# Two forms of a small matrix-vector product at the head of a two-layer diffusion trunk

## The chip, the cores and the metric

The kernel runs on one core of a Trainium2 chip. The metric is the device time of one execution in microseconds (us). The core's engines work side by side, each through its own list of instructions: TensorE (PE, whose weight loads are shown apart as PEld), VectorE (DVE), ScalarE (ACT), GpSimd (POOL) and SyncE (SP), which issues the transfers from the chip's memory. An engine waits only where an instruction needs what another engine or a transfer has not finished.

## The reference

Two streams of 256 tokens with 1024 features, the latent one (L) and its context (C), pass through two layers of half-step SwiGLU, token mixer and half-step SwiGLU. Every sub-layer is preceded by an RMS norm, a scale and a shift, and followed by a gate; these come from one small product per layer, the modulation: two vectors (one per stream) times a 1024 x 9216 matrix, in fp32.

```python
    s_c = jax.nn.silu(c)
    s_cc = jax.nn.silu(c_ctx)[None]
    for i in range(DEPTH):
        ...
        ml = (s_c @ w_mod[i] + b_mod[i]).reshape(-1, 3, 3, D)
        h = gated_residual(h, ml, 0, swiglu(ada_in(h, norm_g[i, 0], ml, 0), ffn_w_in[i, 0], ffn_w_out[i, 0]), 0.5)
        ...
            mc = (s_cc @ w_mod[i] + b_mod[i]).reshape(-1, 3, 3, D)
            hc = gated_residual(hc, mc, 0, swiglu(ada_in(hc, norm_g[i, 0], mc, 0), ffn_w_in[i, 0], ffn_w_out[i, 0]), 0.5)

def ada_in(h, g, m, j):
    xn = rms_norm(h, g)
    return (xn * (1.0 + m[:, j, 1][:, None]) + m[:, j, 0][:, None]).astype(h.dtype)
```

## The kernel before, in words

All activations are held with features on the 128 partitions, as eight chunks of 128 features. The large products use a format in which a float32 is split into a high part and a low remainder (`whi`, `wlo` for weights, two `slot` tiles for activations); a product is three matmuls, high by high, high by low, low by high. Weights stream through two `raw` buffers; ACT rounds them to `whi` (a CAST) and DVE subtracts to get `wlo`. `mm` (L259 is its matmul) issues one matmul and then lets a planner, which keeps an estimate of each engine's time, slip background work between matmuls. In the first stage the planner is held off, and the instructions stand in the order in which the code names them.

The change is in that first stage, which ends when the first SwiGLU runs in its steady form. The modulation's columns come in blocks of 512 (`blk`). Shift and scale of the first sub-layer are the blocks 0 to 3: blocks 0 and 2 hold shift and scale of features 0 to 511, blocks 1 and 3 those of 512 to 1023. `start_loads` fetches a block as four quarters (`q`) of 512 KB. `mod` multiplies it, with 1024 inputs as eight chunks `kk`. Before, the vectors are the stationary side: four columns (two vectors and two columns of padding or of low parts) by 512 moving weight columns, which gives a 4 x 512 result.

- Block 0 and the first half of block 2 are plain fp32 (`sT`).
- The other half of block 2 and all of blocks 1 and 3 are first split (`high` on ACT, `low` on DVE), and `s_parts` holds the split vectors; each chunk is two matmuls.
- The result lies along one axis of four rows, so `mod_end` copies it out (ACT) and `turn` turns it with four matmuls against `C_PAIR`, after which two DVE additions write it to `modT`.

The transfers are issued by SP in the order of the calls from L1376: block 0, constants, stream L, block 2, first weight tile, stream C, second weight tile, blocks 1 and 3. Around the products stand the RMS norm of each stream (`first_squares` on ACT, `add_squares` on DVE, `first_rows` as two-column matmuls on TensorE, `rsqrt` as eight small DVE operations, `diagonal`, `columns`), and `norm_steps`, which makes the split activations of one chunk at a time: a DVE product `t`, an ACT step that gives the high part, a DVE step that gives the low part.

`between` then runs the first two weight tiles on features 0 to 511: `half(i, s)` is weight tile i on stream s, 24 matmuls of 256 columns. Its order is half(0, L), half(1, L), the norm of C, half(0, C), `mod(1)`, `mod(3)`, and half(1, C) around their two `turn` steps. The remaining chunks of features (`normed(..., range(4, KC))`) need blocks 1 and 3. All later work is the same code in both kernels.

Of the kernel before, what the change touches and what calls it, by code (L numbers as in the profile page):

```python
# [9 lines left out]
F32 = mybir.dt.float32  # L10
F32R = mybir.dt.float32r
I32 = mybir.dt.int32
AF = mybir.ActivationFunctionType
ALU = mybir.AluOpType
# [3 lines left out]
P = 128  # L18
D = 1024
KC = D // P  # L20
# [8 lines left out]
L, C = 0, 1  # L29
# [5 lines left out]
C_PAIR = 386  # L35
# [36 lines left out]
def trunk(ctx, tc, a):  # L72
    nc = tc.nc

    cpool = ctx.enter_context(tc.tile_pool(name="cpool", bufs=1))
# [13 lines left out]
    def slot(shape, dt=F32):  # L89
        t = slots.tile([P, 1024], dt, tag="slot", name=nm("slot"))  # L90
        dims = dict(zip("abc", shape[1:]))
        names = " ".join(dims)
        flat = t[:, :int(np.prod(shape[1:]))]
        return flat if len(dims) == 1 else flat.rearrange(f"p ({names}) -> p {names}", **dims)
# [9 lines left out]
    def t512(dt=F32):  # L104
        return tmp.tile([P, 512], dt, tag="t512", name=nm("t512"), bufs=5)
# [12 lines left out]
    def one():  # L118
        return ps_one.tile([P, 512], F32, tag="one", name=nm("one"))
# [11 lines left out]
    def account(e, reads, writes, us):  # L131
        start = now[e]
        for ap in reads:
            t, by = ready.get(key(ap), (0.0, e))
            start = max(start, t + (HOP if by != e else 0.0))
        now[e] = start + us
        for ap in writes:
            ready[key(ap)] = (now[e], e)
# [22 lines left out]
    V = Engine("dve", nc.vector, 0.06, 960.0)  # L161
    A_ = Engine("act", nc.scalar, 0.09, 1200.0)
# [9 lines left out]
    con = cpool.tile([P, C_W], F32, name="con")  # L172
    sT = cpool.tile([P, KC, 4], F32, name="sT")
    vec = cpool.tile([P, 48 + 8 + 16], F32, name="vec")
    bmod = cpool.tile([P, 2, 72], F32, name="bmod")
# [82 lines left out]
    def mm(out, lhsT, rhs, start, stop):  # L258
        nc.tensor.matmul(out, lhsT=lhsT, rhs=rhs, start=start, stop=stop)  # L259
        n = int(np.prod(rhs.shape[1:]))  # L260
        account("pe", [lhsT, rhs], [out], n / 2400.0 * (1 if rhs.dtype == F32R and n >= 256 else 4) + 0.0025)
        advance()
# [47 lines left out]
    def force(tile_no, part, half=1, earlier=True):  # L310


        while True:
            wanted = [x for x in soon if x[1] < tile_no and earlier or x[1] == tile_no and x[3] <= part and x[4] <= half]
            if not wanted:
                return
            soon.remove(wanted[0])
            wanted[0][2]()
# [72 lines left out]

    bg = bg_steps()

    s_parts = cpool.tile([P, KC, 4], F32R, name="s_parts")
    A_.copy(out=s_parts[:, :, 0:2], in_=sT[:, :, 0:2])
    V.tensor_tensor(out=s_parts[:, :, 2:4], in0=sT[:, :, 0:2], in1=s_parts[:, :, 0:2].bitcast(F32), op=ALU.subtract)

    blocks, highs, lows = {}, {}, {}  # L400

    def start_loads(blk):
        for q in range(4):
            blocks[blk, q] = slot([P, 2, 512])
            dma(out=blocks[blk, q], in_=a["wmod"][0, blk, q // 2][:, 2 * (q % 2):2 * (q % 2) + 2, :])

    def high(blk, q):
        highs[blk, q] = slot([P, 2, 512], F32R)
        A_.copy(out=highs[blk, q], in_=blocks[blk, q])

    def low(e, blk, q):
        lows[blk, q] = slot([P, 2, 512], F32R)
        e.tensor_tensor(out=lows[blk, q], in0=blocks[blk, q], in1=highs[blk, q].bitcast(F32), op=ALU.subtract)

    def mod(blk, midway={}):

        ps = one()[0:4, :]
        for q in range(4):
            if q in midway:
                midway[q]()  # L420
            for k in range(2):
                kk = 2 * q + k
                ends = dict(start=kk == 0, stop=False), dict(start=False, stop=kk == KC - 1)
                if (blk, q) in highs:
                    mm(ps, lhsT=s_parts[:, kk, :], rhs=highs[blk, q][:, k, :], **ends[0])
                    mm(ps, lhsT=s_parts[:, kk, :], rhs=lows[blk, q][:, k, :], **ends[1])
                else:
                    mm(ps, lhsT=sT[:, kk, :], rhs=blocks[blk, q][:, k, :], start=kk == 0, stop=kk == KC - 1)
        return lambda: mod_end(blk, ps)

    def mod_end(blk, ps):
        row = t512()
        A_.copy(out=row[0:4, :], in_=ps)

        def turn():
            pt = one()
            for c in range(4):
                mm(pt[:, 2 * c:2 * c + 2], lhsT=row[0:4, c * P:(c + 1) * P], rhs=con[0:4, C_PAIR:C_PAIR + 2], start=True, stop=True)
            for v in range(2):
                V.tensor_tensor(out=modT[:, 0, v, 4 * blk:4 * blk + 4], in0=pt[:, v:8:2], in1=bmod[:, 0, 4 * blk:4 * blk + 4], op=ALU.add)  # L440
                made.add((0, v, blk))

        return turn

    def mcol(l, v, j, w, kk=slice(0, KC)):
        c0 = (j * 3 + w) * KC
# [41 lines left out]
    def first_squares(s, k):  # L488

        sq = t512()  # L490
        A_.activation(out=sq, in_=h[s][:, k:k + 2, :].rearrange("p k t -> p (k t)"), func=AF.Square)
        return sq

    def add_squares(e, acc, sq, eps=0.0):
        e.scalar_tensor_tensor(out=acc, in0=sq, scalar=eps * D / P / 2, in1=acc, op0=ALU.add, op1=ALU.add)
        return acc

    def first_rows(acc):
        ps = one()
        for t in range(2):  # L500
            for i in range(2):
                mm(ps[:, 2 * t:2 * t + 2], lhsT=acc[:, i * S + t * P:i * S + t * P + P], rhs=con[:, C_MEAN:C_MEAN + 2], start=i == 0, stop=i == 1)
        return ps[:, 0:4:2], ps[:, 1:4:2]
# [41 lines left out]
    def norm_steps(l, j, s, xt, bc, ks, kk):  # L545
        aa = tiny.tile([P, KC], F32, tag="scl", name=nm("scl"), bufs=2)
        V.scalar_tensor_tensor(out=aa[:, kk], in0=mcol(l, s, j, 1, kk), scalar=1.0, in1=ng[:, l, j, kk], op0=ALU.add, op1=ALU.mult)
        low = []

        def step(k):  # L550
            if k is not None:
                hi, lo = xt[k // 2]
                o = (slice(None), k % 2, slice(s * S, s * S + S))
                t = t256()
                bb = mcol(l, s, j, 0, slice(k, k + 1))
                V.scalar_tensor_tensor(out=t, in0=h[s][:, k, :], scalar=aa[:, k:k + 1], in1=bc[:, :S], op0=ALU.mult, op1=ALU.mult)
                A_.activation(out=hi[o], in_=t, func=AF.Identity, bias=bb, scale=1.0)
            if low:
                low.pop()()
            if k is not None:  # L560
                low.append(lambda: V.scalar_tensor_tensor(out=lo[o], in0=t, scalar=bb, in1=hi[o].bitcast(F32), op0=ALU.add, op1=ALU.subtract))

        return [lambda k=k: step(k) for k in list(ks) + [None]]
# [827 lines left out]
    def diagonal(s):  # L1391
        diag[s] = rstd_diag(rsqrt(*rows[s]))
# [5 lines left out]
    sums_l = first_squares(L, 0)  # L1398
    for k in range(2, KC, 2):
        add_squares(V, sums_l, first_squares(L, k), EPS if k == 2 else 0.0)  # L1400

    def early():
        rows[L] = first_rows(sums_l)
        turn = end()
        for q in (2, 3):
            high(2, q)
            low(V, 2, q)
        diagonal(L)
        turn()

    end_2 = mod(2, {2: early})
    turn_2 = end_2()
    columns(L)
    turn_2()
    pump()
    xt = norm_tiles()
    force(0, 0, 0)
    sums_c = []
    for i, step in enumerate(norm_steps(0, 0, L, xt, scale[L], range(4), slice(0, 4))):
        step()  # L1420
        if i >= 2:
            sums_c.append(first_squares(C, 2 * len(sums_c)))
    sums_c.append(first_squares(C, 6))
    force(0, 1, 0)

    def between(banks, ws):

        half = lambda i, s, ks=range(4): abreast(xt, s, [(banks[i][s], ws[i])], ks, True)
        half(0, L)
        add_squares(V, sums_c[0], sums_c[1])  # L1430
        add_squares(V, sums_c[2], sums_c[3])
        add_squares(V, sums_c[0], sums_c[2], EPS)
        half(1, L)
        rows[C] = first_rows(sums_c[0])
        diagonal(C)
        for q in range(2):
            high(1, q)
        columns(C)
        for i, step in enumerate(norm_steps(0, 0, C, xt, scale[C], range(4), slice(0, 4))):
            step()  # L1440
            if i >= 2:
                low(V, 1, i - 2)
                if i < 4:
                    high(1, i)
        half(0, C)
        low(V, 1, 3)
        for q in range(4):
            high(3, q)
            low(V, 3, q)
        turn_1 = mod(1)()  # L1450
        force(1, 1)
        turn_3 = mod(3)()
        turn_1()
        half(1, C, range(1))
        turn_3()
        half(1, C, range(1, 4))
        for s in BOTH:
            normed(0, 0, s, xt, scale[s], range(4, KC))
        state["inside"] = False
# [112 lines left out]
```

## Time and profile before

| quantity | value |
|---|---|
| time, median of 3 runs | 1951.71 us (1951.39 to 1952.37) |
| time of the profiled execution | 1952.25 us |
| its span, first to last instruction | 1950.2 us |
| TensorE busy in the span | 1924.2 us (99%) |
| VectorE, ScalarE, GpSimd busy | 1352.0, 687.9, 73.0 us |
| read from memory | 276.11 MB, 142 GB/s over the span |
| mean granted TensorE clock | 0.994 of full speed |

The profiled execution lies 2.05 us outside its span, and 0.54 us above the median. Times in the rows are counted from the span's start. An fp32 matmul stands in the trace as two weight loads and two matmul records, a matmul in the split format as one of each. A busy TensorE is not one that does useful work all the time: the records of consecutive matmuls overlap, so what counts is the distance from start to start.

### The profile page before, as it was taken

The page shows a single profiled execution, that of the slowest core. Times are in us where ns is not written, and L with a number is a line of the kernel's source. Part 1 is how long each engine was busy: PE and PEld are TensorE (multiplying, and loading weights), DVE is VectorE, ACT ScalarE, POOL GpSimd, SP SyncE. Part 2 cuts the span into 40 slices and gives each one's busy share as a digit, 9 for nine tenths or more (in the row PEclk, how much of TensorE's full clock was granted, in tenths as well). Part 3 has the DMA queues.
Part 4 walks back from the last instruction along what each step waited for, and adds up shares of the span by engine and source line. Part 5 has one row for each costly group of instructions (what it writes and reads, how often), then busy time and mean ns, then how long its engine had stood idle before and what let it go on. Part 6 is the DMA issues. An engine that isn't in the chain of part 4 may idle for free.

```text
span 1950.2 us, 26148 instructions
## 1 busy us (share of the span) xinstructions
PE 1924.2 (99%) x10458; PEld 1661.8 (85%) x10458; DVE 1352.0 (69%) x2402; ACT 687.9 (35%) x1035; POOL 73.0 (4%) x108
## 2 busy tenths in 40 slices
PE   7999999999999999999999999999999999999998
PEld 4888888898888888888888889888888899989998
DVE  5576666678788888876666676767632588887665
ACT  5422232333323232342222223322222366665443
POOL 1000000010000000100000000000000101100000
PEclk8999999999999999999999999999999999999999
DMA  7334534434434434234353343555433345544553
GB/s 287 141 137 129 187 130 136 156 119 151 142 133 141 147 130 142 86 130 149 125 179 132 140 139 98 194 189 200 162 101 82 110 119 113 98 115 167 194 176 114
DMA packets 70090, 278.85 MB, mean 143 GB/s; under 512 B 23632, under 2 KB 23888, under 8 KB 52304
## 3 DMA queue, kind: packets, MB, share of 16 engines
q1 hardware_dynamic: 69968, 277.18, 43.5%
q8 instruction: 82, 1.34, 0.3%
q14 instruction: 40, 0.33, 0.0%
HBM read 276.11 MB, written 1.05 MB: 142 GB/s over the span
## 4 chain that ended last, share of the span: by engine, by line
PE 94%; DVE 3%; ACT 2%; DMA 1%; issue 0%; SPq 0%; DVEq 0%; ACTq 0%
PE pair L259 61%; PE one L259 32%; DVE slot L151 1%; PE one L265 1%; DMA slot<-in_wmod 1%; DVE t L151 1%; ACT slot L151 1%; DVE wlo L151 1%; ACT whi L151 1%; DVE few L151 0%; DMA raw<-in_nv 0%; ACT t L151 0%; DVE h L151 0%; PE pair L265 0%; SPq L166 0%
## 5 line engine op out<-in xcount | busy, mean ns | idle before, releaser
L259 PE MATMUL pair<-slot,whi 128*128 128x512 f32 (+2 forms) x4000 | 1039.1, 351 | 6.8 <-ACT slot L151 4.7
L259 PEld LDWEIGHTS pair<-slot,whi 128*128 128x128 f32 x4000 | 696.4, 190 | 104.3 <-ACT slot L151 5.4
L259 PE MATMUL pair<-slot,wlo 128*128 128x512 f32 (+2 forms) x2000 | 682.5, 350 | 0.1
L259 PE MATMUL one<-slot,whi 128*128 128x512 f32 (+1 forms) x1860 | 481.4, 347 | 0.0
L151 DVE TENSOR_TENSOR wlo<-raw,whi 128x1024 fp32r<-128x1024 f32 (+1 forms) x400 | 436.4, 1122 | 38.5 <-ACT whi L151 37.7
L151 ACT CAST whi<-raw 128x1024 fp32r<-128x1024 f32 (+1 forms) x400 | 365.0, 959 | 225.3 <-PE one L259 138.6
L259 PEld LDWEIGHTS pair<-slot,wlo 128*128 128x128 f32 x2000 | 372.9, 190 | 48.8 <-DVE wlo L151 0.4
L259 PEld LDWEIGHTS one<-slot,whi 128*128 128x128 f32 x1860 | 325.9, 189 | 43.4
L259 PE MATMUL one<-slot,wlo 128*128 128x512 f32 (+1 forms) x930 | 323.1, 347 | 0.0
L151 DVE SCALAR_TENSOR_TENSOR acc<-mraw,sT,acc 128x512 f32<-128x512 f32 x392 | 279.2, 750 | 17.1 <-DMA mraw<-in_wmod 15.9
L151 ACT ACTIVATE t<-pair 128x512 f32<-128x512 f32 x66 | 39.4, 597 | 442.9 <-PE pair L259 442.9
L259 PEld LDWEIGHTS one<-slot,wlo 128*128 128x128 f32 x930 | 176.1, 189 | 21.8
L151 DVE TENSOR_TENSOR t<-pair,t 128x512 f32<-128x512 f32 x66 | 45.6, 692 | 204.2 <-ACT t L151 204.2
L151 DVE TENSOR_TENSOR slot<-t,slot 128x512 fp32r<-128x512 f32 (+2 forms) x144 | 88.1, 612 | 64.8 <-ACT slot L151 63.4
L151 ACT CAST slot<-t 128x512 fp32r<-128x512 f32 (+2 forms) x144 | 79.4, 552 | 122.1 <-DVE t L151 121.7
L151 DVE SCALAR_TENSOR_TENSOR h<-one,gate,h 128x256 f32<-128x256 f32 x112 | 49.6, 479 | 103.6 <-PE one L259 103.4
L151 POOL TENSOR_TENSOR t<-t,t 128x256 f32<-128x256 f32 x47 | 39.4, 850 | 1708.4 <-ACT t L151 1286.9
L259 PE MATMUL pair<-whi,slot 128*128 128x512 f32 (+1 forms) x384 | 98.5, 339 | 0.0
L259 PE MATMUL one<-slot,slot 128*128 128x512 f32 (+1 forms) x432 | 89.8, 348 | 1.3 <-DVE slot L151 1.0
L151 ACT ACTIVATE t<-h 128x256 f32<-128x256 f32 (+1 forms) x88 | 36.9, 434 | 142.8 <-DVE h L151 129.3
L259 PEld LDWEIGHTS one<-slot,slot 128*128 128x128 f32 x432 | 69.9, 189 | 10.8 <-DVE slot L151 1.4
L259 PEld LDWEIGHTS pair<-whi,slot 128*128 128x128 f32 x384 | 67.2, 189 | 7.5
(100 smaller groups left out, 1077.8 us busy)
## 6 DMA issues: line engine op xcount, KB each, us to landing
raw<-in_win SPq DMA_DIRECT2D x88, 1024.0 KB, 4.9
mraw<-in_wmod SPq DMA_DIRECT2D x128, 512.0 KB, 4.7
raw<-in_wout SPq DMA_DIRECT2D x64, 704.0 KB, 4.2
slot<-in_wmod SPq DMA_DIRECT2D x16, 512.0 KB, 10.3
raw<-in_rv SPq DMA_DIRECT2D x8, 1024.0 KB, 4.8
raw<-in_rg SPq DMA_DIRECT2D x8, 1024.0 KB, 4.9
raw<-in_ro SPq DMA_DIRECT2D x8, 1024.0 KB, 4.9
slot<-in_ex SPq DMA_DIRECT2D x8, 512.0 KB, 6.0
```

Of the source, the lines that this page charges most:

```text
L151: getattr(self.real, op)(*args, **kw)
L259: nc.tensor.matmul(out, lhsT=lhsT, rhs=rhs, start=start, stop=stop)
L265: nc.tensor.transpose(out=out, in_=in_, identity=ident)
```

## The change

`mod` now makes the weights the stationary side: for each chunk and each 128 of the block's 512 columns, the 128 x 128 piece of weights is loaded, and the two vectors move past it, in plain fp32. That is 32 matmuls of two columns per block, and the result stands on the partitions as `modT` wants it. `s_parts`, `high`, `low`, `mod_end` with its copy, and the turning matmuls are gone. The order is written anew: `early` (the row sums of stream L) comes before the second quarter of block 2; the squares of C follow all norm steps of L; `first_rows` of C and the forced second half of weight tile 0 come before half(1, L); half(1, C) stands whole between `mod(1)` and `mod(3)`.

```diff
-    s_parts = cpool.tile([P, KC, 4], F32R, name="s_parts")
-    A_.copy(out=s_parts[:, :, 0:2], in_=sT[:, :, 0:2])
...
-        ps = one()[0:4, :]
+        ps = one()[:, 0:8]
         for q in range(4):
             if q in midway:
                 midway[q]()
             for k in range(2):
                 kk = 2 * q + k
-                ends = dict(start=kk == 0, stop=False), dict(start=False, stop=kk == KC - 1)
-                if (blk, q) in highs:
-                    mm(ps, lhsT=s_parts[:, kk, :], rhs=highs[blk, q][:, k, :], **ends[0])
-                    mm(ps, lhsT=s_parts[:, kk, :], rhs=lows[blk, q][:, k, :], **ends[1])
-                else:
-                    mm(ps, lhsT=sT[:, kk, :], rhs=blocks[blk, q][:, k, :], start=kk == 0, stop=kk == KC - 1)
-        return lambda: mod_end(blk, ps)
...
+                for c in range(4):
+                    mm(ps[:, 2 * c:2 * c + 2], lhsT=blocks[blk, q][:, k, c * P:c * P + P], rhs=sT[:, kk, 0:2],
+                       start=kk + c == 0, stop=kk == KC - 1 and c == 3)
+                    account("pe", [], [], 0.1)
+
+        def end():
             for v in range(2):
...
+    end()
 
     def early():
         rows[L] = first_rows(sums_l)
-        turn = end()
-        for q in (2, 3):
-            high(2, q)
-            low(V, 2, q)
         diagonal(L)
-        turn()
-
-    end_2 = mod(2, {2: early})
...
+    end = mod(2, {1: early})
     columns(L)
...
         add_squares(V, sums_c[0], sums_c[2], EPS)
+        rows[C] = first_rows(sums_c[0])
+        force(1, 1, 0)
+        diagonal(C)
         half(1, L)
...
         half(0, C)
...
-        turn_1 = mod(1)()
+        mod(1)()
         force(1, 1)
-        turn_3 = mod(3)()
-        turn_1()
-        half(1, C, range(1))
-        turn_3()
-        half(1, C, range(1, 4))
+        half(1, C)
+        mod(3)()
```

From the steady first SwiGLU on, every engine has the same instructions in the same order. The head of TensorE's list before, where `one_168` is the result of block 0, `one_188` that of block 2, `one_193` the row sums of L, and `one_221` the turned block 0:

```order
L259 MATMUL one_168<-slot_97,sT 4x512 x2
L259 MATMUL one_188<-slot_103,sT 4x512 x2
L259 MATMUL one_188<-slot_105,sT 4x512 x2
L259 MATMUL one_193<-con,t_27_177 128x2 x4
L259 MATMUL one_221<-con,t_33_198 128x2 x4
L259 MATMUL one_188<-slot_200,s_parts 4x512
L259 MATMUL one_188<-slot_202,s_parts 4x512
```

The same head in the changed kernel, with block 0 as `one_165`, block 2 as `one_211`, the row sums as `one_220`, and `one_262` the norm factors of L spread over the partitions:

```order
L259 MATMUL one_165<-sT,slot_94 128x2 x8
L259 MATMUL one_211<-sT,slot_100 128x2 x8
L259 MATMUL one_220<-con,t_27_198 128x2 x4
L259 MATMUL one_211<-sT,slot_102 128x2 x8
L259 MATMUL one_211<-sT,slot_104 128x2 x8
L259 MATMUL one_211<-sT,slot_106 128x2 x8
L259 MATMUL one_262<-t_35_235,con 128x128 x2
```

A quarter of a block was two fp32 matmuls of 512 columns, or four split ones; it is now eight of two columns, and the turn is gone. The row sums stand one quarter earlier.

The end of the stage on TensorE, changed kernel: `one_431` is block 1, `one_494` block 3, `pair_308` with `whi_269` and `wlo_270` is half(1, C), and `pair_307<-slot_275` the first matmul on features 512 to 1023.

```order
L259 MATMUL one_431<-sT,slot_120 128x2 x8
L259 MATMUL pair_308<-slot_271,whi_269 128x256
...
L259 MATMUL pair_308<-slot_273,wlo_270 128x256 x4
L259 MATMUL one_494<-sT,slot_122 128x2 x8
L259 MATMUL one_494<-sT,slot_124 128x2 x8
L259 MATMUL one_494<-sT,slot_126 128x2 x8
L259 MATMUL one_494<-sT,slot_128 128x2 x8
L259 MATMUL pair_307<-slot_275,whi_267 128x256
```

Before, half(1, C) stood behind both blocks and closed the stage; now block 3 stands directly ahead of the first matmul that needs it.

On DVE in the changed kernel, around the norm of C: `t_54_299` is the sum of its squares, `few_349` the start of `rsqrt`.

```order
L151 SCALAR_TENSOR_TENSOR t_54_299<-t_56_303,t_54_299 128x512
L151 TENSOR_TENSOR wlo_268<-raw_109,whi_267 128x1024
L151 TENSOR_TENSOR wlo_270<-raw_112,whi_269 128x1024
L151 TENSOR_SCALAR few_349<-one_336 128x2
```

Before, one such subtraction stood between the sums and `rsqrt`; now there are two, and the ten subtractions of `low` are gone.

## Rows read from the trace of the kernel before

**Rows 1.** Busy time by stretch (start:end, length, engines; last: clock, DMA, GB/s).

```profile
34.16:37.57 3.41, 1.47 (x11) 1.22 (x11) 1.83 (x11) 0.00 (x0) 0.00 (x0) 1.00 1.01 402
37.57:47.81 10.24, 8.18 (x30) 6.04 (x30) 9.99 (x14) 7.58 (x10) 0.00 (x0) 0.50 0.02 8
54.64:58.05 3.41, 3.41 (x28) 3.24 (x28) 0.95 (x7) 0.38 (x1) 0.00 (x0) 1.00 0.81 320
58.05:61.47 3.42, 3.42 (x19) 3.42 (x18) 3.00 (x9) 1.93 (x4) 0.00 (x0) 0.50 0.67 271
61.47:1940.00 1878.53, 1872.40 (x10231) 1630.63 (x10231) 1312.80 (x2313) 655.97 (x987) 64.40 (x79) 1.00 0.43 139
```

**Rows 2.** TensorE in order of time (start, length, operation, count, wait before it).

```profile
5.21 12.96 PE L259 MATMUL one<-slot,sT 128*4 128x512 f32 x24 [5.21 <-DMA slot<-in_wmod]
...
25.49 3.96 PE L259 MATMUL pair<-slot,whi 128*128 128x256 f32 x16 [1.51 <-ACT slot L151]
...
33.99 0.95 PE L259 MATMUL one<-con,t 128*128 128x2 f32 x8
...
44.28 1.91 PE L259 MATMUL pair<-slot,wlo 128*128 128x256 f32 x8
45.98 8.42 PE L259 MATMUL one<-slot,s_parts 128*4 128x512 f32 x32
...
56.22 1.05 PE L259 MATMUL one<-con,t 4*128 4x2 f32 x8
57.20 2.27 PE L259 MATMUL pair<-slot,whi 128*128 128x256 f32 x12
...
60.55 0.63 PE L259 MATMUL pair<-slot,whi 128*128 128x256 f32 x2
...
62.05 0.40 PE L259 MATMUL pair<-slot,whi 128*128 128x256 f32 x2
...
72.12 0.40 PE L259 MATMUL pair<-slot,whi 128*128 128x256 f32 x2
```

**Rows 3.** Groups of instructions up to 63 us (count, busy us, mean ns, idle).

```profile
L259 PE MATMUL one<-slot,s_parts 128*4 128x512 f32 x40 | 10.4, 419 | 0.0
L259 PE MATMUL one<-con,t 4*128 4x2 f32 x32 | 4.2, 249 | 0.0
```

**Rows 4.** Weight loads in order of time, single ones and one merged stream.

```profile
9.43 0.13 PEld L259 LDWEIGHTS one<-slot,sT 128*4 128x4 f32 x1 [0.72 <-issue]
10.28 0.09 PEld L259 LDWEIGHTS one<-slot,sT 128*4 128x4 f32 x1 [0.72 <-issue]
10.71 0.09 PEld L259 LDWEIGHTS one<-slot,sT 128*4 128x4 f32 x1 [0.34 <-issue]
...
14.32 0.08 PEld L259 LDWEIGHTS one<-slot,sT 128*4 128x4 f32 x1 [0.52 <-DMA slot<-in_wmod]
...
33.88 0.98 PEld L259 LDWEIGHTS one<-con,t 128*128 128x128 f32 x8
...
43.47 0.29 PEld L259 LDWEIGHTS pair<-slot,whi 128*128 128x128 f32 x1 [0.60 <-DVE slot L151]
43.64 0.33 PEld L259 LDWEIGHTS pair<-slot,whi 128*128 128x128 f32 x1
```

**Rows 5.** ACT and DVE in order of time, around the two norms.

```profile
18.18 1.04 ACT L151 CAST slot<-slot 128x1024 fp32r<-128x1024 f32 x1 [0.27 <-DMA slot<-in_wmod]
...
24.02 0.23 DVE L151 TENSOR_TENSOR modT<-one,bmod 128x4 f32<-128x4 f32 x2 [1.45 <-PE one L259]
...
24.41 0.87 DVE L151 SCALAR_TENSOR_TENSOR t<-h,scl,one 128x256 f32<-128x256 f32 x2
...
28.25 1.22 DVE L151 TENSOR_TENSOR wlo<-raw,whi 128x1024 fp32r<-128x1024 f32 x1
29.38 2.01 DVE L151 SCALAR_TENSOR_TENSOR t<-t,t 128x512 f32<-128x512 f32 x3
...
37.63 0.87 DVE L151 SCALAR_TENSOR_TENSOR t<-h,scl,one 128x256 f32<-128x256 f32 x2 [0.54 <-PE one L259]
```

More of the change, by code (lines that the diff above doesn't have):

```diff
@@ L392, in trunk @@
     bg = bg_steps()
-    s_parts = cpool.tile([P, KC, 4], F32R, name="s_parts")
-    A_.copy(out=s_parts[:, :, 0:2], in_=sT[:, :, 0:2])
-    V.tensor_tensor(out=s_parts[:, :, 2:4], in0=sT[:, :, 0:2], in1=s_parts[:, :, 0:2].bitcast(F32), op=ALU.subtract)
-    blocks, highs, lows = {}, {}, {}
+    blocks = {}
     def start_loads(blk):
@@ L405, in start_loads @@
             dma(out=blocks[blk, q], in_=a["wmod"][0, blk, q // 2][:, 2 * (q % 2):2 * (q % 2) + 2, :])
[L407 to L413, printed above, removed]
     def mod(blk, midway={}):
-        ps = one()[0:4, :]
+        ps = one()[:, 0:8]
         for q in range(4):
@@ L422, in mod @@
                 kk = 2 * q + k
-                ends = dict(start=kk == 0, stop=False), dict(start=False, stop=kk == KC - 1)
-                if (blk, q) in highs:
-                    mm(ps, lhsT=s_parts[:, kk, :], rhs=highs[blk, q][:, k, :], **ends[0])
-                    mm(ps, lhsT=s_parts[:, kk, :], rhs=lows[blk, q][:, k, :], **ends[1])
-                else:
-                    mm(ps, lhsT=sT[:, kk, :], rhs=blocks[blk, q][:, k, :], start=kk == 0, stop=kk == KC - 1)
-        return lambda: mod_end(blk, ps)
[L431 to L438, printed above, removed]
+                for c in range(4):
[3 more added lines that the diff above has]
+        def end():
             for v in range(2):
-                V.tensor_tensor(out=modT[:, 0, v, 4 * blk:4 * blk + 4], in0=pt[:, v:8:2], in1=bmod[:, 0, 4 * blk:4 * blk + 4], op=ALU.add)
+                V.tensor_tensor(out=modT[:, 0, v, 4 * blk:4 * blk + 4], in0=ps[:, v:8:2], in1=bmod[:, 0, 4 * blk:4 * blk + 4], op=ALU.add)
                 made.add((0, v, blk))
-        return turn
+        return end
     def mcol(l, v, j, w, kk=slice(0, KC)):
@@ L1400, in trunk @@
         add_squares(V, sums_l, first_squares(L, k), EPS if k == 2 else 0.0)
+    end()
     def early():
         rows[L] = first_rows(sums_l)
-        turn = end()
-        for q in (2, 3):
-            high(2, q)
-            low(V, 2, q)
         diagonal(L)
-        turn()
-    end_2 = mod(2, {2: early})
-    turn_2 = end_2()
+    end = mod(2, {1: early})
     columns(L)
-    turn_2()
+    end()
     pump()
@@ L1417, in trunk @@
     force(0, 0, 0)
-    sums_c = []
-    for i, step in enumerate(norm_steps(0, 0, L, xt, scale[L], range(4), slice(0, 4))):
+    for step in norm_steps(0, 0, L, xt, scale[L], range(4), slice(0, 4)):
         step()
-        if i >= 2:
-            sums_c.append(first_squares(C, 2 * len(sums_c)))
-    sums_c.append(first_squares(C, 6))
     force(0, 1, 0)
+    sums_c = [first_squares(C, k) for k in range(0, KC, 2)]
     def between(banks, ws):
@@ L1432, in between @@
         add_squares(V, sums_c[0], sums_c[2], EPS)
+        rows[C] = first_rows(sums_c[0])
+        force(1, 1, 0)
+        diagonal(C)
         half(1, L)
[L1434 to L1437, printed above, removed]
         columns(C)
-        for i, step in enumerate(norm_steps(0, 0, C, xt, scale[C], range(4), slice(0, 4))):
+        for step in norm_steps(0, 0, C, xt, scale[C], range(4), slice(0, 4)):
             step()
[L1441 to L1444, printed above, removed]
         half(0, C)
[L1446 to L1449, printed above, removed]
-        turn_1 = mod(1)()
-        force(1, 1)
-        turn_3 = mod(3)()
-        turn_1()
-        half(1, C, range(1))
-        turn_3()
-        half(1, C, range(1, 4))
+        mod(1)()
+        force(1, 1)
+        half(1, C)
+        mod(3)()
         for s in BOTH:
```

## The prediction

> **What bounds the kernel now.** I read the busy time by stretch first. From 61.47 us on TensorE is busy in 1872.4 of 1878.5 us [rows 1], and from there every engine has the same list in both kernels. So the change is worth the shift of the moment at which TensorE reaches the first matmul on features 512 to 1023, 60.55 us before [rows 2], and of what the clock does just behind it; nothing later has slack to absorb a delay. Second, TensorE in order of time, to see what that moment hangs on. Two chains lead there: block 0, block 2 and norm of L up to the first wide matmul at 25.49; then half(0, L), half(1, L), norm of C, half(0, C) up to the modulation at 45.98 [rows 2]. Third, the weight loads, since the added matmuls are little else.
>
> **What goes and what comes on TensorE.** Gone are 24 records of the plain four-column form (12.96 us) [rows 2], 40 of the split form (10.4) and 32 turning ones (4.2) [rows 3], together 27.6 us. Added are 4 x 32 fp32 matmuls, 256 records, each with a full weight load and two columns. The form stands in the trace as the row sums: eight loads 0.98 us long, one taking 0.19, so they start 0.113 apart [rows 4], in a stretch whose granted clock is 1.00 [rows 1]. At that pitch a block is 64 x 0.113 = 7.2 us.
>
> At the lower level (1.2 GHz) there is no such row. The nearest is a pair of loads of the same size at 43.47 and 43.64, 0.17 apart [rows 4], clock 0.50 [rows 1]. The bounds are 0.113 (the clock doesn't matter) and 0.226 (all of it doubles); I take 0.17, the measured pair, and a block is 10.9 us. A wide split matmul is 0.120 at the high level (84 records from 62.05 to 72.12 [rows 2]) and 0.213 at the low one (eight in 1.91, the last 0.415 long [rows 2]).
>
> In the Trainium skill, "TensorE: Matmul & The Clock Gate", section "LDWEIGHTS (loading the stationary operand)", a load takes its columns divided by 1.2 in ns, 107 ns for 128, with no word of the gate. The trace agrees at the high level (0.113) and not at the low one (0.17); by the rule the sum would be that of rival 2.
>
> **Which level.** The first records start at the low level: 9.43 to 10.28 is 0.85 us for a record that takes 0.43 from 10.28 on [rows 4], so 5.1 us of wide work from 5.21 on raised the clock. It then falls after narrow work even without a gap: from 54.64 to 58.05 TensorE was busy all 3.41 us, with eight two-column records from 56.22 to 57.20 in it [rows 2], and from 58.05 the clock is 0.50 [rows 1]; wide work alone (256 or 512 columns), from 57.20, brought it back at 61.47, 4.3 us. So I take it that two-column streams let the clock fall and don't raise it, and blocks 0 and 2, now all of that form, never leave the low level. After the last wide work at 33.99 [rows 2] the high level lasted to 37.57 [rows 1], 3.6 us.
>
> The Trainium skill, same page, section "Why this matters for your kernels", asks that TensorE be kept busy without gaps to reach and hold the high clock. By that the gapless two-column streams would hold it, which the stretch before 58.05 contradicts; the time it gives is rival 1.
>
> **Chain of L.** Block 0 from 5.2 (its first quarter lands then) to 16.1. Quarter 0 of block 2 has landed (14.32 [rows 4]): 16 x 0.17 = 2.7, to 18.8. Row sums, 8 x 0.17 = 1.4, to 20.2. Three quarters, 8.2, to 28.4; the last one was in by 18.18 [rows 5], so no transfer is waited for. DVE's `rsqrt` hides under them. `columns` about 0.75, DVE's `t` at 29.2. Before it was at 24.41 and the first wide matmul 1.08 later [rows 2, 5]: now 30.3, which is 4.8 late.
>
> **Chain of C.** Before, `wlo` ended 5.06 after `t` and the sums of C 6.98 after it (28.25 + 1.22, 29.38 + 2.01 [rows 5]). ACT's squares no longer stand between L's steps, which returns 0.3: 34.0 and 35.9. Row sums of C to 37.3, half(1, L) 24 records, 2.9 to 5.1, to 40.2 to 42.4. Moving the row sums ahead of half(1, L) costs TensorE a short wait and buys the chance to hide `rsqrt`; but two `wlo` subtractions stand ahead of it on DVE (35.8 + 1.13 + 1.22 = 38.2), and before it took 2.7 from the row sums' end (33.99 + 0.95) to `t` at 37.63 [rows 2, 5]: 40.9, just as late as TensorE allows (40.2 + 0.75). So `t` of C is at 41.0 to 43.2. half(0, C) took 8.35 from `t` (to 45.98), with two `low` subtractions between the norm steps on DVE and the casts on ACT. Without them it is 1.08 + DVE's pace + 8 low-part matmuls: 5.0 with the clock high, 1.08 + 24 x 0.213 = 6.2 low. That is where taking out `high` and `low` pays, 2.2 to 3.4 us; the rest of them lay beside other work. `mod(1)` starts at 46.0 to 49.3, middle 47.7, against 45.98: 1.7 late.
>
> **End of the stage.** Before, 45.98 to 60.55 = 14.57. Now `mod(1)`: if the clock is high, 3.6 us for 32 records, then 32 x 0.17 = 5.4, together 9.0; if low 10.9; half each, 10.0. half(1, C) at the low level, 24 x 0.213 = 5.1. That is about what raises the clock (4.3 to 5.1), so `mod(3)` begins high in four cases of five: 9.4. Then a new wait: block 3 now stands directly ahead of the matmuls that need it, and what half(1, C) hid lies bare, from `modT` at 24.02 to the first matmul at 25.49, 1.5 us [rows 2, 5]; queued behind that matmul is everything else of TensorE. Sum 26.0, so 11.4 more.
>
> **Behind it.** After `mod(3)` the clock is low, and 4.3 to 5.1 us of wide work raise it: some 22 records x (0.213 - 0.120) = 2.1, less the 0.9 us of that kind that before had too (0.4): 1.7.
>
> **Sum.** 1.7 + 11.4 + 1.7 = 14.8 us on the profiled execution's 1952.25, which is 1950.2 of span and 2.05 around it, and 0.5 above the median of 1951.7. Forecast 1966.5. Its own range, with the two clock states in the middle (3 us down, 4.6 up) and the low pitch 0.02 either way (4 us), is 1959 to 1974.
>
> **Rivals.** I call less than 0.2% either way (1947.8 to 1955.6) the same, since no more can be told.
> 1. *The narrow streams hold the clock.* Place: blocks 0 and 2; it decides if the granted clock is 1.00 from about 10.3. Then block 0 is 30 records at 0.17 and 34 at 0.113, to 14.1; block 2 waits for its load as before (14.32); `t` of L is near 23.7, `t` of C 35.1, half(0, C) ends at 40.1, and 7.2 + 2.9 + 7.2 + 1.5 follow: 58.9, and no slow stretch behind it: 2 us gained, 1949.6, not slower. Against it stands the fall at 58.05; for it, that those narrow matmuls used four rows of the array, and that 1 us of row sums at 33.99 alone shows nothing. 9%.
> 2. *The load doesn't follow the clock.* 0.113 throughout, wide work still slow: `t` of L 23.7, `t` of C near 36.2, half(0, C) to 41.8, then 7.2 + 5.1 + 7.2 + 1.5: 62.8, and 1.7: 3.9 more, 1955.6. Against it the pair at 43.47; for it, that a pair is not a stream. 8%.
> 3. *The narrow records double.* 0.226: 136 records of the L chain, 8 of C's row sums and some 75 of blocks 1 and 3 at 0.055 more, 12 us: 1978.5. For it, that wide records nearly double (0.120 to 0.213). 12%.
>
> **Chances.** Forecast 68%, the rivals 9, 8 and 12, the rest (a wait that I don't see) 3. Leaving out rival 1 and the upper half of rival 3, the range is 1955 to 1978. Faster: a small part of rival 1, 0.04. Same: the rest of it and half of rival 2, 0.10. Slower: 0.86.
>
> **What would show it.** Right: clock 0.50 from the first record up to about 30 us; 64 records of block 0 in about 10.9 us; first wide matmul near 30; `mod(1)` starting near 47.7; a gap of 1.5 us behind `mod(3)`; the first matmul on features 512 to 1023 near 73.7. Wrong: a block in 7.2 us with the clock at 1.00 (rival 1) or 0.50 (rival 2), in 14 us (rival 3), or a transfer that ends a wait in blocks 0 or 2.

## The result, and the profile after

The changed kernel takes 1974.56 us (median of 4 runs, 1973.96 to 1975.11), the one before 1951.9 (4 runs, 1951.39 to 1952.37): a ratio of 1.0117, 95% interval 1.0103 to 1.013. The profiled execution took 1974.81 us, its span 1972.4; against 1952.25 of before that is 22.6 more, where the forecast had 14.8 more and a range that ended at 1978. The direction and the fall of the clock are as forecast; the size, which hangs on what a load costs at the lower level of the clock, is not.

TensorE in order of time in the changed kernel (start, length, operation, count, wait before it):

```profile
5.26 17.20 PE L259 MATMUL one<-sT,slot 128*128 128x2 f32 x80 [5.26 <-DMA slot<-in_wmod]
22.32 1.85 PE L259 MATMUL one<-con,t 128*128 128x2 f32 x8
24.03 10.38 PE L259 MATMUL one<-sT,slot 128*128 128x2 f32 x48
34.27 1.20 PE L259 MATMUL one<-t,con 128*128 128x128 f32 x4
36.58 4.09 PE L259 MATMUL pair<-slot,whi 128*128 128x256 f32 x16 [1.11 <-ACT slot L151]
...
43.38 2.16 PE L259 MATMUL pair<-slot,whi 128*128 128x256 f32 x16
...
48.32 3.38 PE L259 MATMUL pair<-slot,whi 128*128 128x256 f32 x16 [1.11 <-ACT slot L151]
51.54 1.12 PE L259 MATMUL pair<-slot,wlo 128*128 128x256 f32 x8
52.49 10.68 PE L259 MATMUL one<-sT,slot 128*128 128x2 f32 x64
63.03 3.47 PE L259 MATMUL pair<-slot,whi 128*128 128x256 f32 x16
66.33 1.12 PE L259 MATMUL pair<-slot,wlo 128*128 128x256 f32 x8
67.29 11.72 PE L259 MATMUL one<-sT,slot 128*128 128x2 f32 x64
80.52 1.10 PE L259 MATMUL pair<-slot,whi 128*128 128x256 f32 x2 [1.51 <-ACT slot L151]
...
94.90 0.63 PE L259 MATMUL pair<-slot,whi 128*128 128x512 f32 x2
```

The reader is to compare three moments with [rows 2]. The first wide matmul is at 36.58, was at 25.49: 11.1 late. `mod(1)` starts at 52.49, was 45.98: 6.5 late, so 4.6 were given back between the two. The first matmul on features 512 to 1023 is at 80.52, was 60.55: 20.0 late. A further 2.4 comes behind it: from there to the next stage's first matmul (94.90) pass 14.38 us, before 11.93 (60.55 to 72.48). From that matmul to the end of the span both kernels take the same, 1877.5 and 1877.7 us. On TensorE no transfer ends a wait after the first record.

Busy time by stretch (start:end, length, PE, PEld, DVE, ACT, POOL; then clock, DMA share, GB/s), which answers to [rows 1]:

```profile
52.49:55.75 3.26, 3.26 (x32) 3.26 (x31) 0.00 (x0) 0.00 (x0) 0.00 (x0) 1.00 0.00 0
55.75:63.03 7.28, 7.28 (x37) 7.28 (x36) 0.00 (x0) 0.00 (x0) 0.00 (x0) 0.50 0.00 0
...
65.99:69.40 3.41, 3.41 (x32) 3.41 (x31) 0.00 (x0) 0.00 (x0) 0.00 (x0) 1.00 0.65 271
69.40:86.47 17.07, 15.56 (x72) 15.24 (x72) 6.78 (x19) 3.72 (x8) 0.00 (x0) 0.50 0.00 1
86.47:1960.00 1873.53, 1866.98 (x10191) 1625.66 (x10190) 1309.20 (x2304) 654.13 (x984) 63.48 (x79) 1.00 0.43 140
```

`mod(1)` begins with the granted clock at 1.00 and loses it after 3.26 us, with TensorE busy in all of them; from 69.40, 2.1 us into `mod(3)`, and over the wait behind it the clock is at 0.50. From 86.47 on the clock is back at 1.00, as from 61.47 before. The first change of the clock that this trace records is at 42.10, to 1.00; what stands ahead of it has to be read from the records themselves. The weight loads, the first two singly, the first 80 merged, and `mod(1)` on either side of the fall (start, length), which answers to [rows 4]:

```profile
5.23 0.29 PEld L259 LDWEIGHTS one<-sT,slot 128*128 128x128 f32 x1 [5.23 <-issue]
5.39 0.34 PEld L259 LDWEIGHTS one<-sT,slot 128*128 128x128 f32 x1
...
5.23 17.14 PEld L259 LDWEIGHTS one<-sT,slot 128*128 128x128 f32 x80 [5.23 <-issue]
...
52.49 3.33 PEld L259 LDWEIGHTS one<-sT,slot 128*128 128x128 f32 x29
55.62 7.46 PEld L259 LDWEIGHTS one<-sT,slot 128*128 128x128 f32 x35
```

Over the first 80 loads the distance is 0.213 (17.14 less one load of 0.29, over 79). In `mod(1)` it is 0.11 while the clock reads 1.00 (29 in 3.33) and 0.21 while it reads 0.50 (35 in 7.46). So the stream from 5.23 on ran at 1.2 GHz. The first two loads start 0.16 apart but end 0.21 apart (5.52 and 5.73): only the start of the second is early.

DVE around the norms, which answers to [rows 5]:

```profile
35.51 0.87 DVE L151 SCALAR_TENSOR_TENSOR t<-h,scl,one 128x256 f32<-128x256 f32 x2 [0.71 <-PE one L259]
...
42.27 2.35 DVE L151 TENSOR_TENSOR wlo<-raw,whi 128x1024 fp32r<-128x1024 f32 x2
44.54 0.15 DVE L151 TENSOR_SCALAR few<-one 128x2 int32<-128x2 int32 x1
...
47.24 0.87 DVE L151 SCALAR_TENSOR_TENSOR t<-h,scl,one 128x256 f32<-128x256 f32 x2 [0.60 <-PE one L259]
...
79.05 0.23 DVE L151 TENSOR_TENSOR modT<-one,bmod 128x4 f32<-128x4 f32 x2 [14.48 <-PE one L259]
```

`t` of L is at 35.51 (24.41 before), `t` of C 11.73 later (13.22 before). The step `rsqrt` of C begins at 44.54, behind the two `wlo`. And 14.48 us in which DVE waits for TensorE end with block 3's result at 79.05.

### The profile page after: what moved, and what is told of

Same layout as the page of the kernel before. It is cut to its first block, busy times and chain, and to the rows that moved or that the text cites. A ratio compares the mean times of both kernels' runs of the same rounds, so it can differ in the third digit from the quotient of the medians.

```text
span 1972.4 us, 26437 instructions
## 1 busy us (share of the span) xinstructions
PE 1947.9 (99%) x10618; PEld 1703.8 (86%) x10618; DVE 1339.8 (68%) x2391; ACT 676.0 (34%) x1020; POOL 70.7 (4%) x108
## 4 chain that ended last, share of the span: by engine, by line
PE 95%; DVE 2%; ACT 1%; DMA 1%; issue 0%; DVEq 0%; SPq 0%; ACTq 0%
PE pair L259 61%; PE one L259 34%; PE one L265 1%; DVE slot L151 1%; DVE t L151 1%; DVE wlo L151 1%; ACT whi L151 0%; ACT slot L151 0%; DMA raw<-in_wout 0%; DMA raw<-in_nv 0%; DVE h L151 0%; DMA slot<-in_wmod 0%; ACT t L151 0%; DVE few L151 0%; PE pair L265 0%
```

## The experiments

Theory A: the price is TensorE's clock; streams of two moving columns leave it at 1.2 GHz or let it fall there, and that doubles the distance of the loads. Theory B: the price is the 256 full weight loads as such. Theory C: the price is the new order, above all block 3 directly ahead of the matmuls that need it. All six kernels compute the whole of the reference. The first four were timed on one chip together (before: 1951.88, 15 runs), the last two on another (1951.63, 18 runs).

**The same loads with 128 moving columns.** The moving side is the two vectors repeated 64 times; order, loads and their number are those of the changed kernel.

```diff
+    MW = 128
...
-        ps = one()[:, 0:8]
+        ps = one()[:, 0:4 * MW]
...
-                    mm(ps[:, 2 * c:2 * c + 2], lhsT=blocks[blk, q][:, k, c * P:c * P + P], rhs=sT[:, kk, 0:2],
...
+                    nc.tensor.matmul(ps[:, MW * c:MW * c + MW], lhsT=blocks[blk, q][:, k, c * P:c * P + P], rhs=s_wide[:, kk, :],
...
+    s_wide = slot([P, KC, MW])
+    V.tensor_copy(out=s_wide.rearrange("p k (n v) -> p k n v", v=2), in_=sT[:, :, 0:2].unsqueeze(2).broadcast_to([P, KC, MW // 2, 2]))
```

> The changed kernel with one size altered: the moving side of the 128 modulation matmuls is 128 columns wide (the two vectors, repeated 64 times by one DVE copy ahead of the stage) in place of 2; the same 256 weight loads, the same order. Theory A (the two-column stream lets the granted clock fall, and the load's pitch is 0.213 us at the low level and 0.112 at the high one): the clock reads 1.00 from about 10 us on, block 0 takes 24 records at 0.213 and 40 at 0.115, 9.7 us, the later blocks about 7.4 each, first wide matmul near 25, time 1948 to 1954 us. Theory B (256 full weight loads are the price, and the clock is a bystander): the records stay 0.21 apart or get slower, time 1974 us or more.

Measured: 1952.95 (1950.67 to 1956.63, 11 runs), ratio to before 1.001 [1.0001, 1.0019]. Of the 22.7 us, 21.6 are gone. TensorE in order of time, and the stretches:

```profile
4.96 11.56 PE L412 MATMUL one<-slot,slot 128*128 128x128 f32 x80 [4.96 <-DMA slot<-in_wmod]
...
24.79 3.96 PE L259 MATMUL pair<-slot,whi 128*128 128x256 f32 x16 [1.13 <-ACT slot L151]
...
40.70 7.31 PE L412 MATMUL one<-slot,slot 128*128 128x128 f32 x64
...
59.53 0.91 PE L259 MATMUL pair<-slot,whi 128*128 128x256 f32 x2 [1.51 <-ACT slot L151]
```

```profile
5.00:9.57 4.57, 4.57 (x21) 4.57 (x22) 0.00 (x0) 0.00 (x0) 0.00 (x0) 1.00 0.95 306
9.57:26.64 17.07, 15.59 (x129) 14.67 (x128) 7.28 (x26) 6.52 (x12) 6.55 (x25) 1.00 1.02 415
...
40.70:47.76 7.06, 7.06 (x66) 7.06 (x65) 0.00 (x0) 0.00 (x0) 0.00 (x0) 1.00 0.02 8
```

Up to 9.57, ahead of the first recorded change, 21 records take 4.57 us, 0.218 each, against 0.213 in the changed kernel (the stretch holds 22 loads, so a record more or less is the whole difference); then the clock goes up and a block takes 7.31, 0.11 a record. 64 times the columns cost nothing at either level, so it is not the moving columns that set the distance; the loads are what the two forms share. With the wide form the clock came up after 9.57 and stayed over `mod(1)`, where the two-column form lost it. It was not at 1.00 throughout, as the expectation had it: two stretches of 3.4 us, from 26.64 and from 60.77, read 0.50. B falls: the loads are all there, and the time is that of before within 1.1 us. The wait of 1.51 behind `mod(3)` is there too, so it isn't what costs 22 us.

**The form alone, in the order of before.** The changed kernel's `mod`, with the calls of the first stage in the order of before. The end of the edit is shown (block 1 and block 3 together, half(1, C) in two pieces behind them); the rest puts the result of block 0, the squares, the row sums and the second half of weight tile 0 back to their places.

```diff
...
-        mod(1)()
+        end_1 = mod(1)
         force(1, 1)
-        half(1, C)
-        mod(3)()
+        end_3 = mod(3)
+        end_1()
+        half(1, C, range(1))
+        end_3()
+        half(1, C, range(1, 4))
```

> The two-column form of the change put into the order of before (row sums of L ahead of quarter 2 of block 2, squares of C between the norm steps of L, row sums of C behind half(1, L), both blocks 1 and 3 ahead of half(1, C)). Theory A (the form carries the loss): t of L near 35.5 as in the changed kernel, t of C 1.7 later, blocks 1 and 3 together 24 us (3.3 at the high level, 98 records at 0.213), then half(1, C) 5.1 with no bare wait behind it: 1973 to 1977 us. Theory C (the new order carries a good part of it): 1965 us or less.

Measured: 1975.88 (1975.56 to 1976.92, 4 runs), ratio 1.0124 [1.011, 1.0138], as A has it. TensorE in order of time, and two stretches:

```profile
4.97 20.61 PE L259 MATMUL one<-sT,slot 128*128 128x2 f32 x96 [4.97 <-DMA slot<-in_wmod]
...
54.36 25.23 PE L259 MATMUL one<-sT,slot 128*128 128x2 f32 x128
...
84.38 0.40 PE L259 MATMUL pair<-slot,whi 128*128 128x256 f32 x2
```

```profile
54.36:56.65 2.29, 2.29 (x24) 2.29 (x22) 0.82 (x1) 0.00 (x0) 0.00 (x0) 1.00 0.72 190
56.65:79.45 22.80, 22.80 (x110) 22.80 (x109) 0.23 (x2) 0.00 (x0) 0.00 (x0) 0.50 0.19 74
```

Without the new order, and without a wait ahead of features 512 to 1023, the loss is there in full: 128 narrow records stand in one stream, and the stretch at 0.50 holds 110 records, where 98 were expected. So the form carries it and C falls as the cause. With this form the new order is rather worth 1.3 us; no run of the one lies among those of the other, though the two intervals overlap.

**The new order, with four plain columns.** The order of the changed kernel, `mod` with the vectors stationary, in plain fp32 for all four blocks (before, only block 0 and half of block 2 were plain, the rest split); ACT's copy and the turn come right behind the block where the changed kernel takes its result.

```diff
...
-                for c in range(4):
-                    mm(ps[:, 2 * c:2 * c + 2], lhsT=blocks[blk, q][:, k, c * P:c * P + P], rhs=sT[:, kk, 0:2], ...)
+                mm(ps, lhsT=sT[:, kk, :], rhs=blocks[blk, q][:, k, :], start=kk == 0, stop=kk == KC - 1)
...
         def end():
+            row = t512()
+            A_.copy(out=row[0:4, :], in_=ps)
+            pt = one()
+            for c in range(4):
+                mm(pt[:, 2 * c:2 * c + 2], lhsT=row[0:4, c * P:(c + 1) * P], rhs=con[0:4, C_PAIR:C_PAIR + 2], ...)
...
```

> The order of the change with the four-column form for all blocks (vectors stationary, 512 moving weight columns, plain fp32, result copied out by ACT and turned by four matmuls at once, so TensorE waits for the copy). Theory A: the clock is at 1.00 from about 10 us, a block is 16 records at 0.427 = 6.8 us plus 1.9 for copy and turn; t of L near 26.6, next steps as long as in the changed kernel, 1953 to 1960 us. Theory C: the order itself costs 10 us or more, 1963 us or more.

Measured: 1960.61 (1960.22 to 1963.5, 5 runs), ratio 1.0049 [1.0036, 1.0061]: just above A's range and below what C asks, so it decides little by itself. TensorE in order of time:

```profile
5.10 9.27 PE L259 MATMUL one<-slot,sT 128*4 128x512 f32 x16 [5.10 <-DMA slot<-in_wmod]
15.88 1.36 PE L259 MATMUL one<-con,t 4*128 4x2 f32 x8 [1.51 <-ACT t L151]
...
47.07 7.03 PE L259 MATMUL one<-slot,sT 128*4 128x512 f32 x16
54.82 1.05 PE L259 MATMUL one<-con,t 4*128 4x2 f32 x8 [0.72 <-ACT t L151]
...
58.85 7.03 PE L259 MATMUL one<-slot,sT 128*4 128x512 f32 x16
66.60 1.05 PE L259 MATMUL one<-con,t 4*128 4x2 f32 x8 [0.72 <-ACT t L151]
...
69.15 0.91 PE L259 MATMUL pair<-slot,whi 128*128 128x256 f32 x2 [1.51 <-ACT slot L151]
```

So this kernel differs from before in more than its order. Blocks 1 and 3 in plain fp32 took 7.03 us each, where the split form of before took 8.42 for both [rows 2]: 5.6 us more on TensorE, and the kernel is 8.7 slower than before. The waits for ACT's copy lie bare too (1.51, 0.72, 0.72), since the turn follows blocks 0, 1 and 3 at once; before, other matmuls stood in between. And the clock was at 0.50 from 16.47 to 19.88 behind the first of these waits and in three stretches later. What the order by itself costs or gives with four columns isn't separated by this run; 10 us or more, as C has it, isn't left for it.

**Block 3 ahead of half(1, C).** Two calls of the changed kernel change places.

```diff
         force(1, 1)
-        half(1, C)
         mod(3)()
+        half(1, C)
```

> The changed kernel with one move: block 3 directly behind block 1, and half(1, C) behind both, as before. Theory A: the 1.5 us wait behind block 3 goes and half(1, C) raises the clock ahead of the steady part (2 us), but all of block 3 (64 x 0.213 = 13.65 in place of 11.6) and half(1, C) (5.1 in place of 4.3) run at the low level: 0.6 us less than the changed kernel, 1973.5 to 1974.5. Theory C (the bare wait and the slow stretch behind it are pure loss): 4 us less, 1970.5 us.

Measured: 1973.38 (1973.0 to 1973.51, 4 runs), ratio 1.011 [1.0096, 1.0124]: 1.2 under the changed kernel. TensorE in order of time:

```profile
53.48 23.99 PE L259 MATMUL one<-sT,slot 128*128 128x2 f32 x128
77.33 3.76 PE L259 MATMUL pair<-slot,whi 128*128 128x256 f32 x16
...
81.91 0.40 PE L259 MATMUL pair<-slot,whi 128*128 128x256 f32 x2
```

The wait of 1.5 is gone, half(1, C) covers it. But `mod(3)` now follows `mod(1)` directly, the clock reads 0.50 from 57.12 to 81.01, and all its 64 records stand at 0.213: it takes about 13.6 where it took 11.7. In all the move was worth 1.2, where A had said 0.6 (the median lies 0.1 under A's range), and C's 1970.5 isn't reached. What the wait by itself is worth the traces don't tell so closely: in this execution the clock also fell ahead of the move, from 43.47 to 46.88 inside half(1, L), which it didn't in the changed kernel's, and `mod(1)` starts 1.0 later (53.48 against 52.49).

**128 columns, and block 3 ahead of half(1, C).** The first and the fourth edit together.

> The 128-column moving side, and block 3 directly behind block 1 with half(1, C) behind both. Theory A: with the clock at 1.00 through the stage the bare wait of 1.5 us is what this order hides, and nothing is given back at the low level; the slow stretch behind the wait (3.4 us at 0.50) shrinks or goes: 1.5 to 3 us less than the 128-column kernel in its order, 1949.9 to 1951.5 us. Theory C (as with two columns, the order is worth about 1 us or less): 1952 us.

Measured: 1949.55 (1948.5 to 1952.88, 11 runs), ratio 0.999 [0.9982, 0.9999]. TensorE in order of time:

```profile
40.72 14.46 PE L412 MATMUL one<-slot,slot 128*128 128x128 f32 x128
...
57.88 0.40 PE L259 MATMUL pair<-slot,whi 128*128 128x256 f32 x2
```

128 records in 14.46, all at 1.00 (0.11 each), where the fourth kernel took 23.99 for them. The clock reads 1.00 from 9.03 to 60. The wait is covered, and the first matmul on features 512 to 1023 is at 57.88, 2.7 ahead of before. The median lies 0.35 under the range that A gave, and away from C's 1952.

**128 columns, and block 1 into the wait for the norm of C.** Between C's `columns` and half(0, C) TensorE waits for DVE's `t` and ACT's `slot`; `mod(1)` needs neither. The 128-column edit is in it as well; the calls, against the changed kernel:

```diff
+        end_1 = mod(1)
         half(0, C)
-        mod(1)()
+        end_1()
         force(1, 1)
-        half(1, C)
         mod(3)()
+        half(1, C)
```

> As the kernel with the 128-column moving side and block 3 directly behind block 1's place, but block 1's matmuls stand ahead of half(0, C), in the time in which TensorE waits for the norm steps of C (1.1 us idle and 3.38 us for 16 matmuls that take 1.9 without waits), then half(0, C), block 3, half(1, C). Theory A (only TensorE's list bounds the stage once the clock is up): a further 2.4 us less, first matmul on features 512 to 1023 near 55.4, 1947.3 to 1949 us, under both kernels. Rival: DVE's and ACT's steps are the bound there, and the time is that of block 3 first alone, 1950 to 1951.5 us.

Measured: 1946.23 (1945.86 to 1947.86, 8 runs), ratio 0.9972 [0.9962, 0.9983]: 5.4 us under before and 28 under the changed kernel. TensorE in order of time:

```profile
36.38 7.31 PE L412 MATMUL one<-slot,slot 128*128 128x128 f32 x64
43.45 2.15 PE L259 MATMUL pair<-slot,whi 128*128 128x256 f32 x16
...
46.40 7.31 PE L412 MATMUL one<-slot,slot 128*128 128x128 f32 x64
...
56.42 0.40 PE L259 MATMUL pair<-slot,whi 128*128 128x256 f32 x2
```

half(0, C) is through its 16 high-part matmuls in 2.15 where it took 3.38, without the 1.11 ahead of it, since its `slot` tiles are made while block 1 runs. The rival falls, but the forecast isn't met to the end: the first matmul on features 512 to 1023 was expected near 55.4 and is at 56.42, and the median lies 1.1 under A's range. The traced execution was the slowest of the eight (1947.86); in it the row sums of L stand at 17.82, 1.13 later than in the fifth kernel's trace (16.69), which is about what 56.42 is late. Why the other seven are as fast as they are no trace here shows.

## Why the prediction was right in kind and short in size

**Right.** What bounds the kernel: behind the stage both kernels take the same time, and the loss is the shift of the stage's end plus the slow stretch behind it. That the narrow streams here didn't raise the clock and let it fall without a gap: blocks 0 and 2 ran at 0.213 throughout, and `mod(1)` lost the clock after 3.26 us, where 3.6 was put. TensorE was busy in 3.26 of 3.26 us ahead of that fall, and in the first experiment the same loads held the clock with more columns moving. So rival 1 fell. The Trainium skill, "TensorE: Matmul & The Clock Gate", section "Why this matters for your kernels", asks that TensorE be kept busy; by these traces that alone was not enough. The wait behind `mod(3)` is 1.51 as forecast; no transfer is waited for; `rsqrt` of C comes out level with TensorE, as put; half(0, C) took 5.25 from `t` to `mod(1)`, 5.0 forecast for a high clock and 8.35 before.

**The step that failed: "I take 0.17, the measured pair".** The low-level distance of the loads is 0.213, not 0.17. I took the distance of the starts in the pair of [rows 4], which opened its burst, and there the second load starts early: 0.16 in the changed kernel's trace too. The ends of that pair were 0.21 apart (43.47 + 0.29 and 43.64 + 0.33), which is the distance that a stream keeps; the row held the right number and was read wrongly. The measured 0.213 lies inside the bounds that were put, 0.113 to 0.226, near the end that rival 3 had. The wide matmul of 0.213 at the low level, which stood beside the pair, has the same number; nothing here shows why the two should agree. In L's chain the difference is 136 records x 0.043 = 5.9 of the 6.3 us by which the first wide matmul missed its forecast of 30.3. In `mod(3)` it is 45 records, 2.0 us. Rival 2 goes: the load does follow the clock. Rival 3, at 12%, had the mechanism nearly right: the distance goes from 0.11 to 0.213, close to double, not to its 0.226, and the measured 1974.56 lies nearer its 1978.5 than the forecast's 1966.5. That the range of 1955 to 1978 holds the result is owed to the half of rival 3 that was taken into it; the forecast's own range stopped at 1974 (its terms, 4.6 and 4 above 1966.5, add up to 1975.1, by which it would just have held it). The Trainium skill, same page, section "LDWEIGHTS (loading the stationary operand)", has by its formula 107 ns for 128 columns; the trace agrees at the high level alone (0.11).

**What was off by less.** t of L to t of C took 11.73, forecast 11.8 to 14.0: the clock was back at 42.10, so all of C's row sums and half(1, L) ran high; with half(0, C) at its high value the start of `mod(1)` was 4.8 later than put, not 6.3. `mod(1)` took 10.5 (10.0). half(1, C) took 4.26 (5.1), since its last 1.3 us, from 65.99 on, were already high. `mod(3)` with its wait took 13.2 (10.9): besides the 2.0 above, the clock rose at 65.99 inside half(1, C) and was lost at 69.40, so only 2.1 us of `mod(3)` were high and not 3.6. Behind the stage 2.4 were lost (1.7). Term by term, measured less forecast: 4.8 + 0.5 - 0.8 + 2.3 + 0.7 = 7.5 of the 7.8 that are missing.

Two readings about the clock were too narrow. The 4.3 to 5.1 us of wide work that went ahead of a rise was no fixed price: in the changed kernel the clock rose after 2.96 us of half(1, C) (63.03 to 65.99) and, behind the stage, only after 5.95 (80.52 to 86.47). And the stretch of before that ended with the fall at 58.05 held more narrow work than the prediction counted, the turn of block 1 too:

```profile
54.33 1.05 PE L259 MATMUL one<-con,t 4*128 4x2 f32 x8
```

So TensorE had done two bursts of eight two-column records there, the first begun just ahead of the stretch, with 0.9 us of wide work between them. The clock still fell behind narrow work without a gap.

## What to carry to other kernels

In these runs a matmul with a full fp32 weight load and few moving columns cost as much as one with 128, 0.11 us at the high level of the clock and 0.213 at the low one. Price such a matmul at both levels from a stream in the trace, or from the ends of two loads, and not from the starts of a burst's first pair. Ask of each long stretch of narrow records whether the clock stays up in it; if not, moving more columns under the same loads may cost nothing and keep it. And look at the order of calls again when the form has changed: with no copy, no turn and no split to wait for, block 1 fits into the wait for the norm. Whether the form of before could have used that wait was not tried.

## What the runs showed that I had not expected

- 128 moving columns in place of 2 under a 128x128 fp32 load cost the same within the count of one record, 0.218 and 0.213 a record at the low level and 0.11 for both at the high one, and the whole kernel is 21.6 us faster by it.
- The second load of a burst starts 0.16 after the first at the low level and still ends 0.21 after it: 0.34 long, the first 0.29.
- Ahead of the first recorded change of the clock the stretches show 1.00, also where the records are those of the low level (21 in 4.57 us up to 9.57 in the first experiment). There the spacing of the records tells the level, not the column.
- The kernel of the first experiment spreads over 1950.67 to 1956.63, more than any other here. Its profiled run had two stretches at 0.50 that the fifth kernel's, with 1.00 from 9.03 to 60, didn't have. Whether the spread comes from such falls at changing places was not tried.
